# Nine instead of seven gate and up pairs by Strassen's scheme, with the affine step and the sums of x moved

## The chip, the core and the metric

The kernel runs on one core of one Trainium2 chip. TensorE (PE in the profile) multiplies matrices; VectorE (DVE), ScalarE (ACT) and GpSimd (POOL) work element by element; SyncE (SP), and also ACT and POOL, issue DMA transfers. Each engine works through its own instructions strictly in the order in which the program gives them, and waits for the others by semaphores. The metric is device time in microseconds (us) of one execution. The kernel before took 955.36, 956.61 and 959.73 us in three runs, median 956.61.

## The reference

Two decoder layers work on 512 tokens of width 1024 in float32. Layer 0 mixes tokens by causal pooling, layer 1 by differential attention; each mixer is followed by a gated feed-forward block (FFN) with an inner width of 2816:

```python
for i in range(DEPTH):                                   # DEPTH = 2, ALPHA = sqrt(2)
    h = pooling(x) if i % 2 == 0 else diff_attention(x)
    x = layernorm(ALPHA * x + h, ln_mix_g[i], ln_mix_b[i])
    y = (silu(x @ w_gate[i]) * (x @ w_up[i])) @ w_down[i]
    x = layernorm(ALPHA * x + y, ln_ffn_g[i], ln_ffn_b[i])
```

`layernorm` subtracts the mean, divides by the spread, multiplies by a factor per column and adds a shift per column. The last two are the affine step.

## The kernel before, in words

**Products.** Each float32 operand is split into a high part, rounded to the reduced format fp32r, and a low part, the remainder. A product is then three matmuls: high by high, high by low and low by high. The high part is a cast on ACT, the low part a subtraction on DVE, so each block of weights costs one operation on each of the two engines before PE can use it.

**Stages.** Pooling mixer, gate and up stage of FFN 0, its down stage, attention, then gate and up and the down stage of FFN 1. Below, "FFN 0" and "FFN 1" are the two blocks.

**Gate and up stage.** The inner width of 2816 is 22 blocks of 128 columns, and these form 11 pairs k = 0 to 10: blocks k and k + 11. A *plain* pair takes four products of 24 matmuls with 512 columns each (function `plain`, one call for each half of the pair). A pair by Strassen's scheme in Winograd's form (function `strassen`) cuts the pair in quarters and takes seven products P1, Q5, P6, Q3, P7, P2, Q4 of 24 matmuls with 256 columns each. They accumulate in three PSUM banks A, C and B; since later products are added into the same bank, ACT copies the bank out in between (bank A after P1 and after P6, bank C after Q5), and the copy must be done before PE writes that bank again: C for Q3, A for P6 and P7. Strassen's scheme needs sums of weight blocks (DVE, line 569) and of four quarters of x (`sums_of_x`: sums on DVE at 614, 629, 631, 634 and 638, casts on ACT at 617, low parts on DVE at 620, in the tile `xs`). `SPLIT` lists the pairs done in this way: 4 to 10, seven of eleven.

**Start of the stage.** The first 3 blocks (FFN 0) or 2 blocks (FFN 1), called `early`, are computed in two halves of 256 tokens, since the second half of x is still being transposed and split when PE starts (`late`). `advance` prepares weights ahead of PE; there are six buffers for split weights and five for raw ones.

**What else DVE and ACT do in this stage.** `gated` multiplies silu(gate) by up (600, 601); `affine` (200, 201) applies factor and shift of the previous layer norm to the residual rows `res`, as two operations on 128x1024 for each of the four token blocks; `sum_hidden` forms sums of the activations for the down stage (700 to 709); `weight_sums` forms sums of down weights. For the last: for each row of terms k, `load_terms` loads two transfers and one that adds on landing, all on POOL's queue (668, 669), DVE adds twice (674, 675) and ACT's queue writes the result back to memory (679); `load_terms(k + 2)` may start only after that write, since it uses the same tile. The tile of rows 3, 5, 7, 9 and 10 has the tag `gb`, which it shares with the factors and shifts of the layer norm; row 1 uses free rows of the tile `hid`.

**Down stage.** It also runs by Strassen's scheme: seven products P1, Q5, P6, Q3, P7, P2, Q4 of six items each. `prepare` keeps the splitting of weights (d_j for item j, 0 to 41) five items ahead of PE and that of the left operands (into `xs`, a subtraction at line 737 first in product P6) four ahead; then `multiply` issues the item's matmuls, and `add_to` adds each finished product to `res`.

## Time and profile before

| | |
|---|---|
| three timed runs | 955.36, 956.61, 959.73 us |
| the profiled execution: its span, first to last instruction | 952.5 us |
| median of the runs above that span | 4.1 us |
| PE, DVE, ACT, POOL busy in the span | 935.5, 780.4, 490.3, 118.0 us |
| FFN 0: gate and up, from PE's first matmul to its last | 36.4 to 269.5 us |
| FFN 0: down stage, first six products begin and end | 269.5 to 359.3 us |
| FFN 1: gate and up | 606.5 to 836.9 us |

A row of a timeline reads: start and duration in us, engine, line, operation, tiles (output<-inputs), shape, and in brackets the idle time of the engine before the instruction with what ended it. Operations are pipelined, so that the next one of the same engine can start a little before the printed duration is over; what an instruction adds to a busy engine is the distance of the starts. A table of stretches gives for each stretch its length, then for each engine the busy time and in parentheses the number of instructions. In the rows of transfers the last number is the time from issue to landing.

### The profile page before, as it was taken

The page shows a single profiled execution, that of the slowest core. Times are in us where ns is not written, and L with a number is a line of the kernel's source. Part 1 is how long each engine was busy: PE and PEld are TensorE (multiplying, and loading weights), DVE is VectorE, ACT ScalarE, POOL GpSimd, SP SyncE. Part 2 cuts the span into 40 slices and gives each one's busy share as a digit, 9 for nine tenths or more (in the row PEclk, how much of TensorE's full clock was granted, in tenths as well). Part 3 has the DMA queues.
Part 4 walks back from the last instruction along what each step waited for, and adds up shares of the span by engine and source line. Part 5 has one row for each costly group of instructions (what it writes and reads, how often), then busy time and mean ns, then how long its engine had stood idle before and what let it go on. Part 6 is the DMA issues. An engine that isn't in the chain of part 4 may idle for free.

```text
span 952.5 us, 15381 instructions
## 1 busy us (share of the span) xinstructions
PE 935.5 (98%) x5986; PEld 847.0 (89%) x5986; DVE 780.4 (82%) x1134; ACT 490.3 (51%) x788; POOL 118.0 (12%) x148
## 2 busy tenths in 40 slices
PE   8899999999999999999999999999999999999995
PEld 8898899999988888988888888998899999988884
DVE  7859979999988677688777677789779999987777
ACT  6743335555554467665556553833345554654460
POOL 4311211110001201000000000311211110001102
PEclk9999999999999999999999999999999999999998
DMA  9387988875877964333232222396888785868942
GB/s 249 131 275 236 329 254 277 257 238 212 269 244 267 368 223 134 107 89 100 74 126 79 65 89 89 121 321 214 272 240 264 240 281 200 260 242 288 357 136 89
DMA packets 82776, 197.90 MB, mean 208 GB/s; under 512 B 14820, under 2 KB 26724, under 8 KB 82702
## 3 DMA queue, kind: packets, MB, share of 16 engines
q1 hardware_dynamic: 42908, 115.09, 36.5%
q0 software_dynamic: 16192, 47.19, 17.9%
q10 hardware_dynamic: 23602, 34.63, 9.9%
q8 instruction: 47, 0.77, 0.3%
q14 instruction: 27, 0.22, 0.1%
HBM read 159.64 MB, written 36.72 MB: 206 GB/s over the span
## 4 chain that ended last, share of the span: by engine, by line
PE 92%; DVE 3%; ACT 2%; POOL 1%; issue 1%; DMA 1%; POOLq 0%; DVEq 0%
PE A L823 17%; PE P L889 13%; PE C L823 8%; PE Q L889 6%; PE B L823 4%; PE u L127 3%; PE u L125 3%; PE u L126 3%; PE g L126 3%; PE g L127 3%; PE g L125 3%; PE s L1079 2%; PE v L125 2%; PE v L127 2%; PE v L126 2%; PE q L126 2%
## 5 line engine op out<-in xcount | busy, mean ns | idle before, releaser
L569 DVE TENSOR_TENSOR raw<-raw,raw 128x1024 f32<-128x1024 f32 x56 | 68.3, 1219 | 0.5
L107 ACT CAST xs<-hid 128x512 fp32r<-128x512 f32 (+1 forms) x60 | 34.7, 581 | 24.4 <-DVE hid L737 24.4
L219 ACT ACTIVATE y<-pt,bT,gT 128x128 f32<-128x128 f32 x96 | 36.1, 456 | 21.0 <-PE pt L208 19.9
L108 DVE TENSOR_TENSOR xs<-hid,xs 128x512 fp32r<-128x512 f32 (+1 forms) x60 | 38.4, 642 | 7.8 <-ACT xs L107 7.8
L1089 ACT ACTIVATE p<-p,mn 128x128 f32<-128x128 f32 (+3 forms) x64 | 35.3, 553 | 14.9 <-DVE mn L1084 14.9
L601 DVE TENSOR_TENSOR hid<-sg,u 128x512 f32<-128x512 f32 x16 | 11.0, 686 | 29.5 <-PE u L127 18.8
L668 POOL DMA_DIRECT2D b<-in_wall x20 | 14.0, 705 | 170.6 <-DMA tsum<-b 111.0
L729 POOL DMA_DIRECT2D xs<-ssum x24 | 17.4, 726 | 142.7 <-PE Q L889 69.0
L108 DVE TENSOR_TENSOR xt<-y,xt 128x512 fp32r<-128x512 f32 x24 | 16.2, 687 | 16.9 <-ACT xt L107 16.7
L108 POOL TENSOR_TENSOR sql<-sq,sqh 128x512 fp32r<-128x512 f32 x7 | 9.0, 1290 | 165.3 <-ACT sqh L107 165.3
L668 POOL DMA_DIRECT2D hid<-in_wall x24 | 18.8, 827 | 77.5 <-DVE g_36l L575 23.6
L1084 DVE CUSTOM_DVE_ANT_0 p<-s,bias 128x128 f32<-128x128 f32 (+3 forms) x64 | 28.1, 486 | 0.0
L171 POOL TENSOR_SCALAR rs<-mv 128x1 f32<-128x1 f32 x16 | 7.8, 488 | 162.0 <-DVE mv L169 162.0
L705 ACT CAST v<-u 128x512 fp32r<-128x512 f32 x22 | 13.6, 620 | 26.9 <-DVE u L703 26.8
L163 DVE BATCH_NORM_STATS2 st<-res 128x6 f32<-128x512 f32 x32 | 22.2, 694 | 1.1
L849 ACT ACTIVATE sg<-sg 128x512 f32<-128x512 f32 x14 | 8.9, 633 | 26.0 <-DVE sg L842 26.0
L108 DVE TENSOR_TENSOR heads<-k,heads 128x512 fp32r<-128x512 f32 x8 | 5.5, 692 | 20.2 <-ACT heads L107 20.2
L669 POOL DMA_DIRECT2D hid<-in_wall x12 | 14.8, 1235 | 58.5 <-DMA hid<-in_wall 52.3
L617 ACT CAST xs<-hid 128x1024 fp32r<-128x1024 f32 x8 | 8.4, 1050 | 23.9 <-DVE hid L634 11.6
L1103 DVE SCALAR_TENSOR_TENSOR p<-p,sm,p 128x128 f32<-128x128 f32 (+3 forms) x32 | 17.7, 552 | 1.1
L838 DVE TENSOR_TENSOR hid<-C,hid 128x512 f32<-128x512 f32 x14 | 9.7, 691 | 10.8 <-PE C L823 9.6
L107 ACT CAST heads<-k 128x512 fp32r<-128x512 f32 x8 | 4.7, 588 | 26.3 <-PE k L127 26.3
(1118 smaller groups left out, 3742.4 us busy)
## 6 DMA issues: line engine op xcount, KB each, us to landing
raw<-in_wall SPq DMA_DIRECT2D x122, 512.0 KB, 4.5
r<-tsum SPq DMA_DIRECT2D x40, 512.0 KB, 4.4
hid<-in_wall POOLq DMA_DIRECT2D x36, 512.0 KB, 7.2
b<-in_wall POOLq DMA_DIRECT2D x30, 512.0 KB, 5.8
r<-in_wall SPq DMA_DIRECT2D x30, 512.0 KB, 4.9
tsum<-hid ACTq DMA_DIRECT2D x24, 512.0 KB, 5.6
ssum<-v ACTq DMA_DIRECT2D x22, 512.0 KB, 4.0
tsum<-b ACTq DMA_DIRECT2D x20, 512.0 KB, 4.9
```

Of the source, the lines that this page charges most:

```text
L107: nc.scalar.copy(dst_h, src)
L108: (low or nc.vector).tensor_tensor(dst_l, src, dst_h.bitcast(F32), op=ALU.subtract)
L125: nc.tensor.matmul(acc, ah, bh, start=start, stop=False)
L126: nc.tensor.matmul(acc, ah, bl, start=False, stop=False)
L127: nc.tensor.matmul(acc, al, bh, start=False, stop=stop)
L219: nc.scalar.activation(y[:, k, :], pt[:, k * P : (k + 1) * P], AF.Identity, bias=bT[:, n, kk : kk + 1], scale=gT[:, n, kk : kk + 1],)
L569: tt(t, raws[pair[0]], raws[pair[1]], op=ALU.add)
L668: nc.gpsimd.dma_start(out=t[:, j], in_=src[:, j])
L823: nc.tensor.matmul(o, w[:, c], x[:, kk, :], start=p in ("P1", "Q5", "P2") and f + kk + e == 0, stop=p in ("Q4", "Q3", "P2") and (f, kk, e) ...
L889: nc.tensor.matmul(accs[s], x[:, k, r], y[:, c], start=first and k == 0 and e == 0, stop=last and k == m - 1 and e == 2, skip_group_check= ...
L1084: nc.vector.tensor_tensor_reduce(out=p, in0=accs[c][:, :w], in1=biases[h][:, w - 1 :: -1] if w < S else biases[h][:, ::-1], op0=ALU.add, o ...
L1089: nc.scalar.activation(p, p, AF.Exp, bias=mn[:, q, c : c + 1], scale=-1.0, accum_out=sm[:, q, c : c + 1],)
```

## The change

Three things change, in both FFN blocks.

1. `SPLIT` becomes 2 to 10: pairs 2 and 3 are now done by Strassen's scheme too, nine of eleven.
2. `sums_of_x` is now stepped from the start of the stage, beside the first products, and ahead of the last splits of x. Row 1 of the terms moves from `hid` to the tile with the tag `gb`. At the start, the weights are now prepared to block 6 in both FFN blocks (before: 6 in FFN 0, 4 in FFN 1).
3. The affine step leaves the gate and up stage. In the down stage each half block of `res` (128x512) is multiplied by the factor (`gained`) before the first product is added to it, and gets the shift, with the factor ALPHA where that is still to come, at a later place (`shifted`): eight operations of each kind for each FFN block. The factors and shifts of the layer norm before the FFN are loaded at the end of the gate and up stage; those that attention uses are loaded at its start, and for the last layer norm a second time, on POOL's queue, after the last shift.

```diff
-SPLIT = (4, 5, 6, 7, 8, 9, 10)
+SPLIT = tuple(range(2, HALF))
...
                 whole(r2, 0, 0)
-                yield
                 whole(r3, 0, 1)
                 yield
                 whole(r0, 1, 0)
...
-                if k == 1:
-                    t = rows_of[:, :, 4:6, :]
-                elif k % 2 == 0 and k < HALF - 1:
+                if k % 2 == 0 and k < HALF - 1:
                     t = rows_of[:, :, 9:11, :]
...
                         if not lo:
-                            advance(2 * early, True)
+                            advance(6, True)
+                            if (f, i) != (0, 0 if final else 1):
+                                next(sums, None)
                     if lo:
                         advance(2 * f + 6)
                         gated(order[f], *accs[f])
-                        affine(n - 1, f)
                         catch_up()
+                        next(sums, None)
                         if f < 2:
                             weight_sums()
-                            next(sums)
...
                 gated(order[f], *a)
-                if f < SB:
-                    affine(n - 1, f)
                 if f in (3, 5, 7):
                     weight_sums()
-                if f == 3:
-                    load_terms(3)
...
-            load_gb(n)
+            load_gb(n - 1)
...
+            def gained(s, d):
+                c = slice(d * 512, (d + 1) * 512)
+                tt(res[:, s, c], res[:, s, c], gbs[n - 1][:, 0, c], op=ALU.mult)
+
+            def shifted(s, d):
+                c = slice(d * 512, (d + 1) * 512)
+                added = s < 2 or d == 1
+                nc.vector.scalar_tensor_tensor(
+                    res[:, s, c], gbs[n - 1][:, 1, c], ALPHA if added else 1.0, res[:, s, c],
+                    op0=ALU.mult, op1=ALU.add,
+                )
+
+            gains = {
+                ("P1", 1): [(0, 0)], ("P1", 3): [(1, 0)],
+                ("Q5", 0): [(2, 1)], ("Q5", 1): [(3, 1)], ("P6", 3): [(0, 1)], ("P6", 4): [(1, 1)],
+                ("P7", 3): [(2, 0)], ("P7", 4): [(3, 0)],
+            }
+            shifts = {
+                ("Q3", 0): [(0, 1)], ("Q3", 1): [(1, 1)], ("Q3", 2): [(2, 1)], ("P7", 0): [(3, 1)],
+                ("P7", 1): [(0, 0)], ("P7", 2): [(1, 0)], ("P7", 3): [(2, 0)], ("P7", 4): [(3, 0)],
+            }
...
                     multiply(j, accs, range(2))
+                    for s, d in gains.get((p, i), ()):
+                        gained(s, d)
+                    for s, d in shifts.get((p, i), ()):
+                        shifted(s, d)
+                if final and p == "P7":
+                    load_gb(n, nc.gpsimd)
...
+            load_gb(n - 1)
             load_bias(0)
...
-                if h == SB + 1:
-                    load_gb(n)
```

How the instructions now stand, at the three places of which the prediction speaks. In the changed file the same operations have other line numbers: sums of x 613, 627, 629, 632, 636 with low parts at 619 (before 614, 629, 631, 634, 638 and 620), the gated product 600 (601), additions of terms 670 and 671 (674, 675), and the two new operations 890 and 895.

DVE in FFN 0, beside the first products. Before, from the low parts of the weights of blocks 4 and 5 (g_4l, g_5l) over the last four splits of x (xt<-y) to the first gated product:

```order
L575 TENSOR_TENSOR g_4l<-raw_334,g_4h 128x1024
L575 TENSOR_TENSOR g_5l<-raw_378,g_5h 128x1024
L108 TENSOR_TENSOR xt<-y_2_0_621,xt 128x4x128
L108 TENSOR_TENSOR xt<-y_2_1_628,xt 128x4x128
L108 TENSOR_TENSOR xt<-y_3_0_669,xt 128x4x128
L108 TENSOR_TENSOR xt<-y_3_1_676,xt 128x4x128
L601 TENSOR_TENSOR hid_535<-sg_0_803,u_0_540 128x512
L200 TENSOR_TENSOR res<-res,gb_528 128x1024
L201 TENSOR_TENSOR res<-res,gb_528 128x1024
```

And now, from the same place behind g_5l:

```order
L613 TENSOR_TENSOR hid_532<-xt 128x1024 x2
L108 TENSOR_TENSOR xt<-y_2_0_621,xt 128x4x128
L108 TENSOR_TENSOR xt<-y_2_1_628,xt 128x4x128
L108 TENSOR_TENSOR xt<-y_3_0_669,xt 128x4x128
L108 TENSOR_TENSOR xt<-y_3_1_676,xt 128x4x128
L613 TENSOR_TENSOR hid_532<-xt 128x1024 x2
L627 TENSOR_TENSOR hid_532<-hid_532 128x1024
L629 TENSOR_TENSOR hid_532<-hid_532 128x1024
L632 TENSOR_TENSOR hid_532<-hid_532 128x1024
L619 TENSOR_TENSOR xs_533<-hid_532,xs_533 128x1024
L636 TENSOR_TENSOR hid_532<-hid_532 128x1024
L619 TENSOR_TENSOR xs_533<-hid_532,xs_533 128x1024
```

Two sums of x now stand ahead of the last splits of x; six sums and two of the four low parts stand between those splits and the first gated product (line 600), which is the next row.

ACT at the first pair by Strassen's scheme, pair 4 before. From the copy of bank A after P1 to its copy after P6; g_nh are casts of weights, v a cast of `sum_hidden`:

```order
L832 COPY sg_4_0_1369<-A_4_1342 128x512
L572 CAST g_21h<-raw_1183 128x1024
L572 CAST g_22h<-raw_1067 128x1024
L679 DMA tsum_537<-hid_535 128x2x512 x2
L834 COPY hid_535<-C_4_1343 128x2x256
L572 CAST g_23h<-raw_1222 128x1024
L705 CAST v_3_1388<-u_3_1387 128x2x256
L836 COPY hid_535<-A_4_1342 128x2x256
```

And now, pair 2:

```order
L824 COPY sg_2_0_1065<-A_2_1038 128x512
L571 CAST g_13h<-raw_878 128x1024
L571 CAST g_14h<-raw_573 128x1024
L705 DMA ssum_535<-v_0_968 512x1x256
L675 DMA tsum_534<-hid_532 128x2x512 x2
L826 COPY hid_532<-C_2_1039 128x2x256
L571 CAST g_15h<-raw_943 128x1024
L701 CAST v_1_1085<-u_1_1084 128x2x256
L828 COPY hid_532<-A_2_1038 128x2x256
```

The same operations stand ahead of the copy of bank C, and one more transfer issue (ssum<-v).

DVE in the down stage of FFN 0, from item 5: d_jl is the low part of the weights of item j, xs that of a left operand. Before:

```order
L108 TENSOR_TENSOR d_5l<-r_5_2912,d_5h 128x512
L108 TENSOR_TENSOR d_6l<-r_6_2946,d_6h 128x1024
L108 TENSOR_TENSOR xs_536<-hid_535,xs_536 128x256
L108 TENSOR_TENSOR d_7l<-r_7_2979,d_7h 128x1024
L108 TENSOR_TENSOR xs_536<-hid_535,xs_536 128x512
```

And now:

```order
L108 TENSOR_TENSOR d_5l<-r_5_3088,d_5h 128x512
L890 TENSOR_TENSOR res<-res,gb_3200 128x512
L108 TENSOR_TENSOR d_6l<-r_6_3122,d_6h 128x1024
L108 TENSOR_TENSOR xs_533<-hid_532,xs_533 128x256
L108 TENSOR_TENSOR d_7l<-r_7_3155,d_7h 128x1024
L108 TENSOR_TENSOR xs_533<-hid_532,xs_533 128x512
L890 TENSOR_TENSOR res<-res,gb_3200 128x512
```

Two factors (890) are new here; two more stand ahead of d_11l and d_12l, still before the first item of product P6, and the other operations keep their order.

More of the change, by code (lines that the diff above doesn't have):

```diff
@@ L679, in sum_terms @@
                     nc.scalar.dma_start(out=dst[:, j], in_=t[:, j])
-                if k + 2 < HALF - 1 and k != 1:
+                if k + 2 < HALF - 1:
                     load_terms(k + 2)
@@ L781, in plain @@
                     ahead(j + i + 5)
-                    if f >= 3:
-                        next(sums, None)
+                    next(sums, None)
                     catch_up()
                 gated(order[f], *a)
-                if f < SB:
-                    affine(n - 1, f)
                 if f in (3, 5, 7):
                     weight_sums()
-                if f == 3:
-                    load_terms(3)
                 if f % 2:
```

7 lines of the change are left out of this document (3 added, 4 removed).

## The prediction

> **What bounds the kernel now.** I read the page's head and its chain of waits first, then the stretches, then the timelines of single engines.
>
> ```profile
> span 952.5 us, 15381 instructions
> PE 935.5 (98%) x5986; PEld 847.0 (89%) x5986; DVE 780.4 (82%) x1134; ACT 490.3 (51%) x788; POOL 118.0 (12%) x148
> ...
> PE 92%; DVE 3%; ACT 2%; POOL 1%; issue 1%; DMA 1%; POOLq 0%; DVEq 0%
> ```
>
> PE is busy for 98% of the span and makes up 92% of the chain that ends last. There is almost no idle time to win: a change is worth what it takes from PE's work, less what PE then has to wait. Three stretches of FFN 0 show PE's work, a pair by Strassen's scheme, a plain pair, and the first three products of the down stage:
>
> ```profile
> 148.55:168.71 20.16, 20.16 (x171) 20.16 (x169) 19.18 (x24) 10.33 (x13) 2.70 (x3) 1.00 0.88 264
> 84.88:106.64 21.76, 21.76 (x98) 18.02 (x97) 19.59 (x23) 9.17 (x11) 2.70 (x3) 1.00 0.66 204
> 269.51:314.42 44.91, 44.91 (x201) 37.17 (x200) 35.63 (x48) 24.93 (x35) 5.10 (x7) 1.00 0.80 268
> ```
>
> In all three PE (first pair of numbers) is busy without a gap at the full granted clock (1.00). DVE (third) has only 1.0 of 20.16 us to spare in a Strassen pair. So DVE is where a wait can arise.
>
> **The saving.** Two pairs in each of two FFN blocks change from plain, 21.76 us, to Strassen, 20.16 us: 4 x 1.60 = **6.4 us**. It is PE's own work and cannot be hidden. By single matmuls: 96 of 512 columns at 226.7 ns against 168 of 256 columns at 120.0 ns.
>
> [...]
>
> **Entry of FFN 0.** Strassen's first pair now starts at block 4 instead of block 8, and the sums of x must be ready by then. These rows carry the walk along DVE, ACT and PE:
>
> ```profile
> 53.59 0.69 DVE L108 TENSOR_TENSOR xt<-y,xt 128x512 fp32r<-128x512 f32 x1 [1.37 <-ACT xt L107]
> ...
> 65.70 0.69 DVE L674 TENSOR_TENSOR hid<-hid 128x512 f32<-128x512 f32 x1
> 66.43 0.69 DVE L675 TENSOR_TENSOR hid<-hid 128x512 f32<-128x512 f32 x1
> 67.04 1.22 DVE L614 TENSOR_TENSOR hid<-xt 128x1024 f32<-128x1024 f32 x1
> 68.17 1.22 DVE L575 TENSOR_TENSOR g_6l<-raw,g_6h 128x1024 fp32r<-128x1024 f32 x1
> ...
> 81.16 0.42 DVE L700 TENSOR_TENSOR u<-hid 128x256 f32<-128x256 f32 x1
> ...
> 82.76 1.22 DVE L575 TENSOR_TENSOR g_10l<-raw,g_10h 128x1024 fp32r<-128x1024 f32 x1
> ...
> 87.30 1.22 DVE L629 TENSOR_TENSOR hid<-hid 128x1024 f32<-128x1024 f32 x1
> 88.55 1.23 DVE L631 TENSOR_TENSOR hid<-hid 128x1024 f32<-128x1024 f32 x1
> ```
> ```profile
> 49.34 1.51 ACT L219 ACTIVATE y<-pt,bT,gT 128x128 f32<-128x128 f32 x4 [1.04 <-DVE xt L108]
> ...
> 53.58 1.28 ACT L600 ACT_TABLE_LOAD   x1
> 59.77 0.60 ACT L600 ACTIVATE sg<-g 128x512 f32<-128x512 f32 x1 [4.91 <-PE g L127]
> ...
> 88.55 1.05 ACT L617 CAST xs<-hid 128x1024 fp32r<-128x1024 f32 x1 [4.11 <-DVE hid L629]
> ```
> ```profile
> 58.13 0.28 PE L125 MATMUL g<-xt,w2h 128*128 128x256 f32 x1
> ```
>
> From start to start DVE needs 1.14 us for 128x1024 (1.25 where it needs the result just before), 0.61 for 128x512 (0.73 likewise), 1.6 for the four sums of `sum_hidden`. Two sums ahead of the splits of x delay these by 2.27, also through ACT, whose y waits for DVE (row 49.34): the last starts at 53.59 + 2.27 = 55.86 and ends at 56.55. PE reads it from 58.13; no wait.
>
> Then come the other sums: from 56.47 to the end of the last sum 1.13 + 3 x 1.25 + 2 x 1.14 + 1.22 = 8.4, so 64.85; ACT casts it (1.05), loads its table, hidden before (1.28), and does the first silu (0.60). The first gated product starts at 67.85. Up to the addition of terms of row 2, DVE has 11 operations of 128x1024, nine of 128x512 and the four of `sum_hidden`, 11 x 1.14 + 9 x 0.61 + 2 x 0.12 + 1.6 = 19.9 us, and waits some 1.3 for the third silu, which stands behind three casts on ACT: it gets there at 67.85 + 21.2 = **89.0**. The affine steps that stood here (2.4 us each, three up to this place) are no longer in the count; without that the sums of x would come later still.
>
> Row 2 must have landed by then:
>
> ```profile
> 65.61 0.40 ACTq L679 DMA_DIRECT2D tsum<-hid  x1
> 71.09 0.74 POOL L668 DMA_DIRECT2D hid<-in_wall  x1 [6.79 <-DVE g_7l L575]
> hid<-in_wall POOLq DMA_DIRECT2D x2, 512.0 KB, 8.3
> hid<-in_wall POOLq DMA_DIRECT2D x1, 512.0 KB, 7.6
> ```
>
> These are the write of row 0, the loads of row 2 that follow it, 5.5 us later, with their landing (8.3 us) and that of the transfer that adds (7.6). ACT now issues the write behind two casts after the first silu, at 69.8, so the loads go at 75.3, land at 83.6, and the adding one lands at **91.2**. DVE waits 2.2. What stands behind it on ACT:
>
> ```profile
> 98.11 0.60 ACTq L709 DMA_DIRECT2D ssum<-v  x1
> 99.42 1.41 ACTq L679 DMA_DIRECT2D tsum<-hid  x1
> 131.86 0.37 ACTq L679 DMA_DIRECT2D tsum<-hid  x1
> 132.32 0.46 ACTq L679 DMA_DIRECT2D tsum<-hid  x1
> 134.35 0.59 ACT L834 COPY hid<-C 128x512 f32<-128x512 f32 x1 [0.35 <-PE C L823]
> ```
> ```profile
> 84.88 0.39 PE L125 MATMUL g<-xt,g_8h 128*128 128x512 f32 x1
> 131.43 2.88 PE C L823 x24
> ```
>
> Two additions and one sum of weights end at 91.2 + 0.73 + 0.61 + 1.22 = 93.8; the cast g_14h waits for it, and behind it stand three issues (0.60 + 0.37 + 0.46) and the copy of bank C (0.59): 95.8. PE wants bank C for Q3 three products after 84.88, at 93.5: it waits 2.3. The copy of A for P7, behind four operations on DVE and a cast, then comes 0.1 late. From there on the pairs repeat what pairs 4 to 10 did without a wait: a wait of PE gives DVE and ACT the same time back, so it is paid once. Row 3, written after the third silu (82.2), loads at 87.7 and lands at 87.7 + 8.3 + 7.6 = 103.6; DVE adds it after pair 2's last product, past 107. Its cover is 3 us. **Entry of FFN 0: 2.4 us.** Bounds: 0.2 if row 2 is in time, 4.4 if both issues take 1.41.
>
> [...]
>
> **Entry of FFN 1.**
>
> ```profile
> 617.19 0.69 DVE L108 TENSOR_TENSOR xt<-y,xt 128x512 fp32r<-128x512 f32 x1 [1.37 <-ACT xt L107]
> ```
> ```profile
> 620.36 0.28 PE L125 MATMUL g<-xt,w100h 128*128 128x256 f32 x1
> ...
> 652.23 0.39 PE L125 MATMUL g<-xt,g_8h 128*128 128x512 f32 x1
> ```
>
> Here the sums of x stand behind the splits, but the casts of blocks 4 and 5 now stand ahead of the last one; at 1.05 each they delay it from 617.19 to 619.3 at most. It is over at 620.0, and PE reads it from 620.36. From 619.3 to the first Strassen pair are 32.9 us; in FFN 0 from 55.86 to 84.88 only 29.0. These 3.9 us more exceed the 2.4 lacking there: **0**, at most 2.4 if the same transfers are later here.
>
> **The affine step in the down stage.** Sixteen operations of 0.61 for each block. The shifts stand in Q3 and P7, where DVE is ahead. Four factors stand before P6, where it is not:
>
> ```profile
> 279.62 1.23 DVE L108 TENSOR_TENSOR d_6l<-r,d_6h 128x1024 fp32r<-128x1024 f32 x1 [0.26 <-ACT d_6h L107]
> ...
> 305.67 0.69 DVE L108 TENSOR_TENSOR xs<-hid,xs 128x512 fp32r<-128x512 f32 x1 [0.69 <-ACT xs L107]
> ```
> ```profile
> 307.62 0.39 PE L889 MATMUL P<-d_15h,xs 128*128 128x512 f32 x1
> ```
> ```profile
> 269.30 0.33 SPq L150 DMA_DIRECT2D gb<-in_lng  x1
> DMA to landing us min/median/max: 4.4/4.9/6.8
> ```
>
> The left operand of item 15 is ready at 306.36 and used at 307.62, 1.26 of slack. Four factors delay it by 2.44, of which d_6l's wait takes 0.26: PE waits **0.9 us in each block, 1.8** in all. Bounds: 0, if other waits of DVE on ACT take the delay, and 2.4 each. The factors are issued at 269.30 and landed by 276.1; the first is used where d_6l's wait began, at 279.3, so there are 3.2 us of cover, DVE with everything that PE needs next would stand behind it, and what exceeds it would cost one for one. The second load for the last layer norm is issued after P7; P2 lies between, 66 x 226.7 ns = 15.0 us, against 8.3. Attention's load now stands on SP ahead of the position bias instead of behind it; both are small beside the time until DVE uses them, and I count 0.
>
> **Sum.** -6.4 + 2.4 + 0 + 1.8 = -2.2, so the span of 952.5 becomes 950.3. The 4.1 us by which the median of the runs, 956.6, exceeds that span stay: **954.4 us**.
>
> **Rivals.**
> 1. *Row 2 lands in time.* The entry costs 0.2: 952.2. For it: DVE's arrival and the landing are only 2.2 apart. Against: both landings are this kernel's own.
> 2. *Nothing waits.* 956.6 - 6.4 = 950.2. It also needs the slack of item 15 to hold; DVE waits 0.69 on ACT there at every item.
> 3. *Every cover is short by its upper bound*: -6.4 + 4.4 + 2.4 + 4.9 = +5.3, 961.9; partial forms lie between 955 and that.
> 4. *Slower: five raw buffers pace Strassen's new pairs.* Three raw blocks must be there at once, the third being fetched only when g_6l frees a buffer.
>
> ```profile
> raw<-in_wall SPq DMA_DIRECT2D x122, 512.0 KB, 4.5
> ```
>
> g_6l ends near 72.1, so this block lands at 76.6 and is summed at 78.6: 2.0 of cover. It decides from 6.5 us of landing on; at the 8.3 of POOL's loads it costs 1.8 here and as much in the next pair, in both blocks: 954.4 + 7.2 = 961.6. Against: 4.5 is the median of 122.
>
> **Chances.** Forecast 0.45, rivals 0.18, 0.20, 0.10, 0.07. A measurement of this kernel can tell about 0.5%, 4.8 us: faster means under 951.8, slower over 961.4. Rival 2 and a part of rival 1 are faster, 0.28; rival 4 and the end of rival 3 slower, 0.09; the rest, 0.63, the same. The range 949.8 to 958.6 leaves out the upper part of rivals 3 and 4 and the lowest tail.
>
> **What would show it.** Pairs 2 and 3 take 20.16 us of PE's work each. PE waits for ACT's copy of bank C (or A) in pair 2 of FFN 0, about 2.4, and for DVE's xs at item 15 of each down stage, about 0.9; nothing at FFN 1's entry. DVE's addition for row 2 waits about 2 for POOL's transfer. The forecast is wrong if waits appear in later Strassen pairs, if a factor waits for its load, or if pairs 2 and 3 cost other than 20.16.

## The result, and the profile after

| | kernel before | changed kernel |
|---|---|---|
| median of the runs | 956.57 us (9 runs, 954.55 to 960.30) | 951.95 us (9 runs, 951.00 to 954.14) |
| ratio, 95% interval | | 0.995 (0.9935 to 0.9965) |
| profiled execution: span | 952.5 us | 950.5 us, its own time 952.29 |
| PE, DVE busy in the span | 935.5, 780.4 us | 933.1, 818.6 us |

The changed kernel is 4.6 us faster, at the edge of what was called measurable beforehand (4.8): by the prediction's bounds 951.95 is still "the same", 0.15 above "faster", though the interval excludes no change. The forecast was 954.4 (949.8 to 958.6): the sign and the range held, the middle was 2.4 us too high. The page of the changed kernel, its head and its chain of waits:

```profile
span 950.5 us, 16048 instructions
PE 933.1 (98%) x6274; PEld 857.9 (90%) x6274; DVE 818.6 (86%) x1190; ACT 507.5 (53%) x812; POOL 119.0 (13%) x150
...
PE 84%; DVE 9%; ACT 3%; issue 2%; POOL 1%; DMA 1%; ACTq 0%; POOLq 0%; DVEq 0%
```

PE is still busy for 98% of the span, but DVE's share of the chain has gone from 3 to 9%: there are places now where DVE sets the pace.

**Two executions that start alike.** The two profiled spans differ by 2.0 us, the medians by 4.6. Part of this lies ahead of everything that the change touches. These rows of the stretches (granted clock: third number from the end) are of the kernel before, of the changed kernel, and of the changed kernel in a second trace (the run after_2 below):

```profile
10.00:15.00 5.00, 5.00 (x41) 4.65 (x40) 3.67 (x7) 3.52 (x6) 2.55 (x2) 1.00 1.08 356
40.00:42.00 2.00, 2.00 (x19) 2.00 (x18) 1.97 (x4) 1.60 (x5) 0.00 (x0) 1.00 0.00 0
```
```profile
10.00:15.00 5.00, 5.00 (x27) 4.60 (x26) 2.73 (x5) 2.24 (x4) 2.51 (x2) 0.66 1.07 379
40.00:42.00 2.00, 2.00 (x12) 2.00 (x11) 1.97 (x4) 1.97 (x4) 0.00 (x0) 0.50 0.00 0
```
```profile
10.00:15.00 5.00, 5.00 (x40) 4.63 (x39) 3.65 (x7) 3.50 (x6) 2.55 (x2) 1.00 1.07 362
40.00:42.00 2.00, 2.00 (x19) 2.00 (x18) 1.97 (x4) 1.60 (x5) 0.00 (x0) 1.00 0.00 0
```

In the first trace of the changed kernel PE had the full clock neither at 10 to 15 us nor at 40 to 42. Compared by the start of one and the same product, it stood 1.6 us behind the kernel before at 36 us and 2.48 behind at 45. In the second trace it stood 0.01 behind at 55. So the second trace is the one to hold against the kernel before, from there on product by product:

| place (start of the same product) | before | after_2 | what the stretch up to here cost |
|---|---|---|---|
| first half products, 55 us | 55.01 | 55.02 | 0.0 |
| first product of down stage 0 | 269.51 | 267.69 | -3.20 for two pairs, +1.37 |
| down stage 0, behind item 15 | | 1.31 ahead | +0.51 |
| entry of FFN 1 | | 1.16 ahead | +0.15 |
| first product of down stage 1 | | 3.93 ahead | -3.20 for two pairs, +0.43 |
| down stage 1, behind item 15 | | 3.40 ahead | +0.53 |
| end of the span | 952.5 | 949.5 | +0.4 |

The columns add up: -6.4 + 1.37 + 0.51 + 0.15 + 0.43 + 0.53 + 0.4 = -3.0. The four pairs gave what they should. New waits of PE took back 3.0 us of it, in five places, and the end of the program took 0.4. The 0.15 stands in attention; both traces of the changed kernel have it, those of seven, both and both_2 do not, and its cause is open. Pair 2 and pair 3 of FFN 0 and the first three products of the down stage in after_2, which answer to the three stretches shown of before:

```profile
84.89:103.53 18.64, 17.52 (x146) 17.32 (x144) 18.45 (x23) 10.23 (x13) 3.44 (x4) 1.00 0.92 293
103.53:123.69 20.16, 20.16 (x171) 20.16 (x169) 19.61 (x24) 10.14 (x13) 2.43 (x3) 1.00 0.92 298
267.69:313.11 45.42, 45.42 (x201) 37.02 (x199) 36.41 (x51) 23.40 (x33) 5.09 (x7) 1.00 0.78 264
```

The first row holds pair 2 up to its last product, six products of 2.88 us: 17.28 of work, 1.36 of waiting. The second is one Strassen pair from last product to last product: 20.16, as in the pairs before, with 0.55 us of DVE to spare. The third is 0.51 longer than the 44.91 of before.

**Where the waits are.** First the entry of FFN 0, in four timelines of after_2: DVE's, ACT's, POOL's and PE's.

```profile
55.87 0.69 DVE L108 TENSOR_TENSOR xt<-y,xt 128x512 fp32r<-128x512 f32 x1 [1.37 <-ACT xt L107]
...
63.66 1.22 DVE L636 TENSOR_TENSOR hid<-hid 128x1024 f32<-128x1024 f32 x1
...
67.91 0.69 DVE L600 TENSOR_TENSOR hid<-sg,u 128x512 f32<-128x512 f32 x1 [1.89 <-ACT sg L599]
...
89.30 0.69 DVE L670 TENSOR_TENSOR hid<-hid 128x512 f32<-128x512 f32 x1
```
```profile
67.37 0.40 ACTq L675 DMA_DIRECT2D tsum<-hid  x1
...
71.09 0.39 ACTq L675 DMA_DIRECT2D tsum<-hid  x1
...
91.88 0.60 ACTq L705 DMA_DIRECT2D ssum<-v  x1
92.52 1.60 ACTq L675 DMA_DIRECT2D tsum<-hid  x2
94.16 0.58 ACT L826 COPY hid<-C 128x512 f32<-128x512 f32 x1 [1.23 <-PE A L815]
```
```profile
70.74 0.74 POOL L664 DMA_DIRECT2D hid<-in_wall  x1 [9.48 <-DVE hid L670]
77.06 0.72 POOL L664 DMA_DIRECT2D hid<-in_wall  x1 [5.58 <-DMA tsum<-hid]
77.78 1.26 POOL L665 DMA_DIRECT2D hid<-in_wall  x1
```
```profile
93.40 0.28 PE L815 MATMUL A<-xs,g_10l 128*128 128x256 f32 x1
94.80 0.50 PE L815 MATMUL C<-xs,g_11h 128*128 128x256 f32 x2 [1.12 <-ACT hid L826]
```

And from the view of line 665, how long the transfer that adds took to land:

```profile
DMA to landing us min/median/max: 6.7/6.7/6.7
```

The walk along DVE came true to a few tenths: last split of x at 55.87 (forecast 55.86), last sum over at 64.88 (64.85), first gated product at 67.91 (67.85), row 2's addition at 89.30 (89.0). But DVE does not wait there: the transfer that adds was issued at 77.78 and landed 6.7 later, at 84.5, not at 91.2. PE waits for bank C nevertheless, since the three issues on ACT take 0.60 + 1.60 us instead of the 1.43 assumed. It starts at 94.80 what it could have started at 93.52.

The same place in FFN 1, DVE and then PE:

```profile
654.02 0.69 DVE L600 TENSOR_TENSOR hid<-sg,u 128x512 f32<-128x512 f32 x1 [1.28 <-ACT sg L599]
...
667.94 0.68 DVE L832 TENSOR_TENSOR hid<-hid,A 128x512 f32<-128x512 f32 x1
```
```profile
668.67 0.50 PE L815 MATMUL A<-xt,g_14h 128*128 128x256 f32 x2 [0.18 <-DVE hid L832]
```

Between these two DVE rows DVE has no pause at all. It comes 0.3 us late to the subtraction that frees bank A for pair 2's last product.

And item 15 of the down stage: the loads of PE's left operand (LDWEIGHTS in the trace, 0.19 us for one; they wait for xs), and the DVE operation they wait for:

```profile
305.90 0.19 PEld L881 LDWEIGHTS P<-d_15h,xs 128*128 128x128 f32 x1 [0.37 <-ACT xs L107]
...
306.63 0.30 PEld L881 LDWEIGHTS P<-d_15h,xs 128*128 128x128 f32 x2 [0.43 <-DVE xs L108]
```
```profile
305.88 0.69 DVE L108 TENSOR_TENSOR xs<-hid,xs 128x512 fp32r<-128x512 f32 x1 [0.69 <-ACT xs L107]
```

The high half, ACT's, is wanted by the item's first matmul, the low half, DVE's, by the third.

### The profile page after: what moved, and what is told of

It reads as the page before. It is cut to its first block, busy times and chain, and to the rows that moved or that the text cites. A ratio compares the mean times of both kernels' runs of the same rounds, so it can differ in the third digit from the quotient of the medians.

```text
span 950.5 us, 16048 instructions
## 1 busy us (share of the span) xinstructions
PE 933.1 (98%) x6274; PEld 857.9 (90%) x6274; DVE 818.6 (86%) x1190; ACT 507.5 (53%) x812; POOL 119.0 (13%) x150
## 4 chain that ended last, share of the span: by engine, by line
PE 84%; DVE 9%; ACT 3%; issue 2%; POOL 1%; DMA 1%; ACTq 0%; POOLq 0%; DVEq 0%
PE A L815 20%; PE P L881 13%; PE C L815 10%; PE Q L881 6%; PE B L815 5%; PE s L1098 2%; PE v L125 2%; PE v L126 2%; PE v L127 2%; PE q L126 2%; PE q L127 1%; PE q L125 1%; PE k L125 1%; PE k L127 1%; PE k L126 1%
## 5 line engine op out<-in xcount | busy, mean ns | idle before, releaser
L568 DVE TENSOR_TENSOR raw<-raw,raw 128x1024 f32<-128x1024 f32 x72 | 87.8, 1219 | 0.6
L664 POOL DMA_DIRECT2D b<-in_wall x24 | 18.0, 799 | 162.3 <-DMA tsum<-b 93.5
L841 ACT ACTIVATE sg<-sg 128x512 f32<-128x512 f32 x18 | 11.4, 632 | 33.5 <-DVE sg L834 33.5
L664 POOL DMA_DIRECT2D hid<-in_wall x20 | 14.8, 740 | 96.6 <-DMA tsum<-hid 31.2
L826 ACT COPY hid<-C 128x512 f32<-128x512 f32 x18 | 10.6, 586 | 26.8 <-PE C L815 22.9
L665 POOL DMA_DIRECT2D b<-in_wall x12 | 14.7, 1229 | 59.2 <-DMA b<-in_wall 52.7
L830 DVE TENSOR_TENSOR hid<-C,hid 128x512 f32<-128x512 f32 x18 | 12.4, 690 | 10.1 <-PE C L815 8.5
L1098 PE MATMUL s<-heads 64*128 64x256 f32 (+2 forms) x192 | 17.9, 330 | 0.0
```

What stands on the lines that cost most here:

```text
L568: tt(t, raws[pair[0]], raws[pair[1]], op=ALU.add)
L664: nc.gpsimd.dma_start(out=t[:, j], in_=src[:, j])
L1098: nc.tensor.matmul(accs[c][:, :wide], a[r, qs], b[r, :wide], start=i == 0, stop=i == 2)
```

## The experiments

All of them compute the whole reference. Kernels measured together shared the runs of the kernel before, whose median was 955.8 to 956.6 each time.

**Seven pairs again (seven).** What is worth how much: the pairs, or the work that was moved for them?

```diff
-SPLIT = tuple(range(2, HALF))
+SPLIT = tuple(range(4, HALF))
```

> The changed kernel with Strassen's scheme for pairs 4 to 10 only, as before; the moved affine steps, the moved sums of x and the moved loads stay. Theory A (the whole gain is PE's own work in the four pairs, less 0.5 and 0.4 of new waits in pair 2 of the two FFN blocks; the moved steps gain nothing by themselves): it loses 6.4 and wins back 0.9, 5.5 above the changed kernel, 957.4 us, and about 1.0 slower than the kernel before by the waits at item 15. Rival B (a good part of the gain comes from the moved work, the pairs only make use of the room): about 953 to 955, faster than before.

956.87 us, 1.001 of before (0.9998 to 1.0022). Against the changed kernel PE lost 2.66 us in FFN 0 and 2.77 in FFN 1, 5.43 together, which is 6.4 less the waits of 0.5 and 0.4 in pair 2 that went too. In the trace that is theory A to a tenth: the moves gain nothing by themselves. The stretch of plain pair 2 in FFN 0 shows that they leave DVE (third pair of numbers) half idle there, 10.61 of 21.76 us where the kernel before had 19.59; this room is what Strassen's pairs then use:

```profile
83.22:104.98 21.76, 21.76 (x98) 18.02 (x97) 10.61 (x15) 6.22 (x8) 3.74 (x5) 1.00 1.05 346
```

**The entry's DVE work put back (work_back).** Are the moves needed at all?

```diff
                         gated(order[f], *accs[f])
+                        again(f)        # twice: res[:, f] = max(res[:, f], res[:, f])
                         catch_up()
...
                 gated(order[f], *a)
+                if f < SB:
+                    again(f)
```

> The changed kernel with as much DVE work back at the entry as the affine steps were there: after each of the first four gated products of an FFN block two operations of 128x1024 on the residual (the maximum of a value with itself, which changes nothing). The affine steps in the down stage stay. Theory A (DVE is the engine that sets pair 2, so work there is paid one for one once its idle time is used up): DVE has 4 x 2.45 = 9.8 us more ahead of row 2's addition, 1.2 of idle time to give in FFN 0 and 1.8 in FFN 1, so PE waits about 8.6 more in FFN 0 and 8 in FFN 1: 968.5 us. Rival B (the weights' casts run ahead far enough, the affine steps need not have moved): 952 to 954.

974.41 us, 1.019 (1.0176 to 1.0212). PE waited twice in pair 2 of FFN 0, and what it did between the two waits ran at half the clock (the row of the stretches behind the two of PE):

```profile
96.89 0.52 PE L823 MATMUL A<-xs,g_10h 128*128 128x256 f32 x2 [3.87 <-ACT sg L832]
...
105.70 0.80 PE L823 MATMUL C<-xs,g_11h 128*128 128x256 f32 x2 [4.18 <-ACT hid L834]
```
```profile
98.00:100.00 2.00, 2.00 (x12) 2.00 (x11) 1.97 (x2) 0.00 (x0) 0.00 (x0) 0.50 0.81 135
```

Against the first trace of the changed kernel FFN 0 lost 11.8 us and FFN 1 9.6, where 8.6 and 8 were expected. The waits themselves, 8.1 in FFN 0 and 6.6 in FFN 1, are near what theory A says; the clock behind them was in neither theory. With that much DVE work at the entry the nine pairs are 18 us slower than the kernel before: moving the affine steps is what makes them pay. (About 1 of the 18 us is item 15's, since the affine steps stay in the down stage too.)

**The sums of x put back (sums_back).** The same question for the other move, in FFN 0 alone.

```diff
                         if not lo:
                             advance(6, True)
-                            if (f, i) != (0, 0 if final else 1):
+                            if final and (f, i) != (0, 0):
                                 next(sums, None)
...
                         catch_up()
                         next(sums, None)
+                        if not final:
+                            next(sums, None)
```

> The changed kernel with all sums of x of FFN 0 behind its gated products again, two portions after each of the first three and the last one in block 3; FFN 1 stays. Theory A (DVE's queue sets pair 2): 11.9 us of DVE work move from ahead of the first gated product to behind it, the first gated product itself comes some 6.5 us earlier since no cast stands ahead of its silu, 1.2 of idle time are used up, so PE waits about 4 us more in pair 2 of FFN 0, and the clock that is granted after such a wait costs another 1 to 2: 956 to 958. Rival B (the place of the sums is indifferent, only their end counts): 952 to 952.5.

960.03 us, 1.005 (1.0033 to 1.0068). DVE came to row 2's addition at 96.23 (89.30 in after_2, where PE stands within half a us of this run). PE waited 2.94 and 2.90 us in pair 2 and ran at half the clock behind each wait (0.50 from 96 to 98 and from 102 to 104 us). Against after_2, which starts alike, FFN 0 lost 7.9 us. Theory A in kind; both its terms, 4 and 1 to 2, were too small (4.5 more waiting and some 3.3 of clock), the clock's above all, since it was paid twice.

**Row 2's terms made late (row2_late).** Does the chain of the prediction hold, from the landing over DVE and ACT to PE?

```diff
-                for j in range(2):
+                for j in (0, 1, 0, 1) if k == 2 else (0, 1):
                     nc.gpsimd.dma_start(out=t[:, j], in_=src[:, j])
```

> The changed kernel with the two loads of row 2's terms issued twice, one after the other, in both FFN blocks, so that the transfer that adds comes later; the result is the same. In the changed kernel that transfer landed at 85.7 and DVE came to the addition at 90.9, 5.2 later. Theory A (the prediction's chain holds, only the landing was misjudged): two more loads of 4 to 6 us each put the landing at 94 to 97, DVE waits 3 to 6 us there, and PE waits the same for bank C: 3 to 6 us more in FFN 0, 955 to 958 with a like wait in FFN 1 up to 961. Rival B (DVE makes up the wait before PE needs bank C): 952 to 953 with DVE waiting but no longer gap of PE.

956.65 us (951.68 to 960.49). In the profiled execution the last transfer landed at 92.0, and these rows of DVE, PE and the stretches follow:

```profile
92.00 0.69 DVE L670 TENSOR_TENSOR hid<-hid 128x512 f32<-128x512 f32 x1 [2.18 <-DMA hid<-in_wall]
```
```profile
97.61 0.57 PE L815 MATMUL C<-xs,g_11h 128*128 128x256 f32 x2 [3.50 <-ACT hid L826]
```
```profile
98.00:100.00 2.00, 2.00 (x11) 2.00 (x11) 2.00 (x3) 1.55 (x3) 0.00 (x0) 0.50 1.00 202
```

DVE waits 2.18, as long as was forecast for the changed kernel itself, and PE 3.50 where after_2 had 1.12, 2.4 more: the chain holds link by link. What follows costs 1.6 us on top: the product behind the wait takes from 97.61 to 102.08, 4.47 us instead of 2.88. In FFN 1 the doubled loads still landed in time, and PE waits as little as in the changed kernel. The shortest run, 951.68, is as short as the changed kernel's own. So the forecast's entry of 2.4 was the price of a lateness that the changed kernel does not have in its two traces.

**Four raw buffers (raws4).** The prediction's fourth rival.

```diff
-RAWS = 5
+RAWS = 4
```

> The changed kernel with four raw buffers instead of five, which fetches each raw block later. It tests the prediction's fourth rival, that the buffers pace Strassen's new pairs. Theory A (the buffers have room to give: nothing in the trace of the changed kernel waits for a raw block in pairs 2 and 3): less than 2 us more, 952 to 954. Rival B (the fetch of the third block of a pair decides, 2.0 us of cover by the prediction): every Strassen pair waits, 18 pairs with 1 us or more, 970 or more.

957.78 us, 1.0025 (1.0009 to 1.0041): neither theory's number. One DVE sum in pair 2 of FFN 0 waits for a raw block, and PE behind it; the other Strassen pairs show no gap that the changed kernel does not have. A second wait stands in the last down stage. DVE and PE in pair 2:

```profile
102.64 1.23 DVE L568 TENSOR_TENSOR raw<-raw,raw 128x1024 f32<-128x1024 f32 x1 [2.54 <-DMA raw<-in_wall]
```
```profile
105.65 0.51 PE L815 MATMUL A<-xt,g_14h 128*128 128x256 f32 x2 [2.02 <-DVE hid L832]
```

Against the first trace of the changed kernel PE lost 2.4 us in pair 2 (1.6 against after_2, whose start is the nearer one), 1.9 late in the last down stage, and some 1.0 in smaller waits of the two down stages. Five buffers cover the new pairs, and in pair 2 of FFN 0 one less is too few: the rival's mechanism exists, at one place, and at five buffers it does not decide.

**The factors twice (factors_twice).** Is item 15's wait DVE's queue, one for one?

```diff
                     for s, d in gains.get((p, i), ()):
                         gained(s, d)
+                        if p in ("P1", "Q5"):
+                            z = res[:, s, d * 512 : (d + 1) * 512]
+                            tt(z, z, z, op=ALU.max)
```

> The changed kernel with each of the four factors ahead of P6 followed by one more operation of 128x512 on the same half row (the maximum of a value with itself, which changes nothing): 4 x 0.61 = 2.44 us more DVE work ahead of item 15's left operand in each down stage. Theory A (DVE runs there without a pause, so PE waits one for one): the wait of 0.52 grows to 2.96 in each stage, 4.9 us in all, 956.8. Rival B (the 0.52 is the handover from ACT, not DVE's queue): within 1 us of the changed kernel.

958.87 us (957.41 to 962.38). PE lost 2.90 and 2.92 us more in the two down stages, where 2.44 each were put in. The delay shows at item 12 already and grows to item 15, whose row has

```profile
313.12 0.50 PE L881 MATMUL P<-d_15h,xs 128*128 128x512 f32 x1 [1.02 <-ACT xs L107]
```

One for one, and some 0.1 us for each left operand that PE waits for: the matmul at 313.12 is followed by the next 0.34 us later, the same one in both, which waits for nothing, 0.23 later (306.75 to 306.98). Theory A. The median is 2.1 us above its 956.8; 0.9 of that lies in these stages, the rest is not explained by the trace, whose own execution (961.73) came to 45 us later than any other.

**Three edits of order (both), the same and one more (held).** Can the new waits be had back by order alone?

```diff
-                ("Q5", 0): [(2, 1)], ("Q5", 1): [(3, 1)], ("P6", 3): ...
+                ("P6", 2): [(2, 1), (3, 1)], ("P6", 3): ...     # Q5's additions right behind these
...
-                yield                      # sum_terms, ahead of the writes
+                for _ in range(1 + later): yield                # later = 1 for row 2
...
-                    catch_up()             # plain(f), second half
-                gated(order[f], *a)
+                gated(order[f], *a)
+                catch_up()
```

> The changed kernel with three edits of order: Q5's additions to the residual and their two factors stand behind the left operand of item 17 instead of ahead of that of item 15; the write of row 2's sums is issued one product later on ACT; the gated product of block 3 stands ahead of the steps that catch up instead of behind them. Theory A (the new waits are DVE's and ACT's order at three places, 0.5 us at item 15 in each down stage, 0.5 in pair 2 of FFN 0, 0.4 in that of FFN 1): all of them go, 1.9 us less than the changed kernel, 950.1. Rival B (PE waits for the same thing a product later, since DVE is busy throughout there): within 0.5 of the changed kernel, with new waits at Q3's first items or in pair 3.

949.98 us, 0.994 (0.9929 to 0.9952). Against the first trace of the changed kernel PE gained 0.51 at item 15 in each down stage, 0.43 in FFN 1's pair 2, all of both, but only 0.13 in FFN 0's, where 0.40 were left, 0.31 of it now in front of the last product. The edit in held, on top of these, starts the sums of block 1's hidden rows behind the subtraction that frees bank A instead of ahead of it:

```diff
-                if f % 2:
+                if f % 2 and k != 1:
                     behind.append(sum_hidden(k))
...
+                    if k == 2 and p == "P7":
+                        behind.append(sum_hidden(1))
```

> The kernel with the three edits of order (both) and one more: the sums of block 1's hidden rows, five DVE operations of 2.2 us together with their wait, start in pair 2 behind the subtraction that frees bank A instead of ahead of it. Theory A (the 0.3 us that PE still waited in pair 2 of FFN 0 are DVE's queue alone): this wait goes too, 949.7 us, no gap of PE over 0.35 us in pair 2 of either block. Rival B (DVE only pays later): a gap of the same size in pair 3.

952.20 us, 0.9966 (0.9953 to 0.9978). The wait in pair 2 is gone in both blocks, and the same wait stands in pair 3, larger, in both:

```profile
125.10 0.50 PE L818 MATMUL A<-xt,g_21h 128*128 128x256 f32 x2 [0.45 <-DVE hid L835]
```

Rival B. DVE has 0.55 us to spare in such a pair; 2.2 us that are put off from one pair come due in the next.

**Side by side (after_2, both_2), and with matmuls in PE's early waits (hot).**

```diff
-        for i in range(11):
+        for i in range(15):                      # the first warming matmuls
...
+            if layer == 0:
+                for _ in range(5):
+                    nc.tensor.matmul(accs[0][0][:, 0:P], ident, ident, start=True, stop=True)
```

> The changed kernel once more, beside the two below on the same chip. Two things are read from it: its time beside theirs, 951 to 953 us, and a second trace of the same program. Theory A (the first 45 us differ from execution to execution by the clock that PE is granted there, and this is why the profiled span of the changed kernel was only 2.0 us shorter than that of the kernel before and not 4.5): PE comes to the same product at 45 us up to 2.5 us earlier or later than in the first trace, with the granted clock below 1.00 in the stretches 10 to 15 us or 36 to 44 us where it comes late, and from there to the end the distances repeat to 0.3 us. Rival B (the 2.5 us belong to the change): the same delay again.

> The kernel with the three edits of order, once more, beside the changed kernel. Theory A: its trace showed 1.8 us less waiting behind the first 45 us, so its time is 1.8 below that of the changed kernel in the same call, 950 us. Rival B (the 2.0 us between the two medians were another day's chip): within 0.5 us of it.

> The same three edits, and matmuls whose results nobody reads in two of PE's early waits: four more of the first warming ones at the start, and five ahead of FFN 0's first product, into a bank that this product starts anew. Theory A (the clock falls to half where PE has waited, and the early waits do this in most executions): the granted clock stays at 1.00 in the stretches 10 to 15 and 36 to 44 us, 1 to 2 us less than without, 948 to 949, and less spread. Rival B (what counts there is the data that come late, or the matmuls added stand in the way): no less than without, or up to 1 us more.

Changed kernel 951.75 (950.17 to 954.69), three edits 949.45 (948.45 to 950.90), with the matmuls besides 950.68 (949.39 to 952.32). after_2 bears out theory A in its first half: the first 45 us are no part of the change. It is wrong in that the rest repeats to 0.3 us: pair 2 of FFN 0 waited 1.36 here and 0.53 in the first trace, where PE came 2.5 us later and DVE, at row 2's addition, only 1.6. The three edits are 2.3 below the changed kernel, measured side by side. The matmuls added gained nothing that can be seen. Their clock stayed at 1.00 in both stretches, but so it did in after_2 and both_2, so this execution does not say whether they hold it. In both_2, which starts as early as after_2, PE waits in pair 2 of FFN 0 again, in two places:

```profile
96.64 0.50 PE L818 MATMUL A<-xs,g_12h 128*128 128x256 f32 x2 [0.30 <-ACT hid L831]
...
103.10 0.51 PE L818 MATMUL A<-xt,g_14h 128*128 128x256 f32 x2 [0.44 <-DVE hid L835]
```

1.16 us in all, hardly less than after_2's 1.36, and hot, which starts as early, waits 1.17: with an early start DVE's queue decides there, and these edits of its order do not help. A third wait of both_2 stands at item 33 of the last down stage, 0.8 us in all, for a left operand's low half, made by DVE:

```profile
915.61 0.73 PE L884 MATMUL P<-d_33h,xs 128*128 128x512 f32 x2 [0.52 <-DVE xs L108]
```

So these two traces end only 0.4 us apart (949.5 and 949.1). hot, with the same three edits and without that wait, ends at 947.6, which is nearer to what the medians say.

**The affine steps of P7 moved into Q3 (tail).** In both_2 the span ends 12.2 us behind the start of PE's last matmul (936.86 of 949.1; before: 941.38 of 952.5, 11.1). From d_27 in the last down stage DVE had no pause to the end of the program, apart from the layer norms' own waits for POOL; ahead of it it had waited for casts of late loads, in after_2 and then both_2:

```profile
889.77 1.23 DVE L108 TENSOR_TENSOR d_25l<-r,d_25h 128x1024 fp32r<-128x1024 f32 x1 [1.28 <-ACT d_25h L107]
892.42 1.23 DVE L108 TENSOR_TENSOR d_26l<-r,d_26h 128x1024 fp32r<-128x1024 f32 x1 [1.43 <-ACT d_26h L107]
894.88 1.23 DVE L108 TENSOR_TENSOR d_27l<-r,d_27h 128x1024 fp32r<-128x1024 f32 x1 [1.23 <-ACT d_27h L107]
```
```profile
894.78 1.23 DVE L108 TENSOR_TENSOR d_27l<-r,d_27h 128x1024 fp32r<-128x1024 f32 x1 [2.93 <-ACT d_27h L107]
```

That DVE's queue sets the end shows in a constant distance: in both, both_2, held and hot the span ends 54.3 us behind the start of d_27l on DVE (894.05, 894.78, 895.85, 893.32), though PE's last matmul stands 11.1 to 12.2 us ahead of the end. How far PE is ahead does not depend on its early start alone: in hot PE's last matmul comes earliest of all, at 936.53, and the end is 11.1 behind it; d_27l waited 1.45 us for its cast there and 2.93 in both_2.

The edit fills these waits, on top of the three edits of order:

```diff
-                ("P7", 3): [(2, 0)], ("P7", 4): [(3, 0)],                    # factors
+                ("Q3", 3): [(2, 0)], ("Q3", 4): [(3, 0)],
...
-                ("Q3", 0): [(0, 1)], ("Q3", 1): [(1, 1)], ("Q3", 2): [(2, 1)], ("P7", 0): ...  # shifts
+                ("Q3", 0): [(0, 1)], ("Q3", 1): [(1, 1), (2, 1)], ("Q3", 2): [(3, 1), (0, 0)],
+                ("Q3", 3): [(1, 0), (2, 0)], ("Q3", 4): [(3, 0)],
```

> The three edits of order (as in both) and, in both down stages, the five shifts and the two factors of product P7 moved into Q3's items, where DVE waited 1.2 to 2.9 us for each of the casts of d_25 to d_27. In the traces of the changed kernel DVE has no pause from d_27 in the last down stage to the end of the program, and where PE comes early the span ends up to 1.1 us later behind PE's last product (12.2 against 11.1 us). Theory A (DVE's queue, filled by the moved affine steps, sets the end of the program in the fast executions): 4.6 us less on it there, PE's last product and the end of the span are 10.9 to 11.1 apart again, and the time is 0.5 to 1.5 below that of the three edits, 948 to 949. Rival B (the casts' weights come late from memory and PE waits for them with or without the shifts): within 0.5 us of 949.5 to 950, with the gap of PE at d_33 still there in some executions.

948.59 us (948.32 to 950.27), 0.9925 of before (0.991 to 0.994): the lowest median, but against the kernel before, measured together, no better than both_2 (0.9923). PE's last matmul starts at 937.79 of 948.3, 10.5 ahead of the end, and DVE has pauses again, waiting for ACT or PE:

```profile
904.78 1.23 DVE L108 TENSOR_TENSOR d_32l<-r,d_32h 128x1024 fp32r<-128x1024 f32 x1 [1.23 <-ACT d_32h L107]
...
922.58 0.69 DVE L871 SCALAR_TENSOR_TENSOR res<-res,P 128x512 f32<-128x512 f32 x1 [0.49 <-PE P L884]
```

So DVE's queue no longer sets the end alone, which is theory A's mechanism. The size of the gain is not shown. This execution starts 2.4 us late, like both's (1.9 late), where the distance was 11.1: 0.5 us are gone, not 1.1, and no trace of this edit starts early, where both_2's 12.2 stood. The times do not tell 948.6 from 949.5 either, since the runs overlap.

## Why the prediction was right, and where it was not

**The saving of 6.4: right.** A Strassen pair took 20.16 in the new places too, and seven lost 5.43 = 6.4 - 0.97.

**Entry of FFN 0, 2.4: the mechanism was right in its second half, wrong in the first; 1.4 with an early start, 0.5 with a late one.** The failing step is "ACT now issues the write behind two casts after the first silu, at 69.8, so the loads go at 75.3, land at 83.6, and the adding one lands at 91.2". The first half of row 0's write went right behind the silu, at 67.4; each half of row 2's load waits only for its own half of the write (the first was issued at 70.74, ahead of the second write at 71.09); the halves landed in 5.1 and 3.9 us, not 8.3; and the adding transfer needs the first half alone, so it was issued 0.7 behind the second load. Four small steps, each taken at its dear end, made 6.7 us. That was rival 1 (row 2 lands in time). That its 952.2 is the result within 0.3 is luck: it lacks 1.2 here, 0.55 at FFN 1's entry and in attention and 0.4 at the end, and has 0.8 too much in P6 and 1.6 outside the span. It gave 0.2 for the rest of this entry, and the rest was 1.4: here the size of the three issues on ACT was off, 2.20 for 1.43, and DVE stood 0.3 later. Why the loads were quicker was not tested. (Beside row 2's loads in before the trace shows reads of one other kind, five loads of raw blocks issued one after the other from 69 to 84 us, and two writes.) Row 3 landed in time too, at 107.7 for an addition at 110.8, the 3 us of cover that were forecast, but by other terms: its adding transfer took 14.3 us (12.7 in the first trace). The memory's traffic in after_2 was down there: 127 GB/s from 65 to 75 us, 265 and 236 in the two halves of the same stretch before.

**Entry of FFN 1, 0: 0.4.** The step "These 3.9 us more exceed the 2.4 lacking there" compared only with row 2. Row 2 was in time; what was late by 0.3 is DVE's own queue, begun 1.28 late since ACT's silu stood behind an issue. With the three edits of order it is gone; that the one that puts the gated product first did it was not tested alone.

**P6, 0.9 in each block: 0.5 in each.** DVE's delay was right, 2.03 where 2.18 were forecast (306.57 against 306.36 for the same low half, with the stage's begin 1.82 earlier). The failing step is "is ready at 306.36 and used at 307.62, 1.26 of slack". The low half, the one that DVE makes, is first read by the item's third matmul, 0.45 later: 1.71 of slack, 0.32 of wait, and 0.2 for the two operands waited for, some 0.1 each (305.90 to 306.24, 0.34 us where 0.23 stand in both).

**Shifts "in Q3 and P7, where DVE is ahead": right in down stage 0, not in the last.** There DVE goes on into the last layer norms with nothing behind it to hide, so the end waits for DVE where its casts come late: 0.4 us in after_2, 1.1 in both_2, nothing in hot. None of the steps priced this.

**The 4.1 us outside the span "stay": 2.45 with an equal start.** An execution's own time exceeded its span by 1.8 (952.29 to 950.5). The other 2.3 us of the 4.1 were most likely the early start of the profiled execution of before, 952.5 + 1.8 = 954.3 against the median of 956.6; there is no second trace of that kernel to show it. With its chain PE's, it should pay a late start in full, as seven did, which carried its 1.5 us to its last item with nothing added but item 15's waits (2.55 there). The changed one pays less: with a start 2.46 us later its span was only 1.0 longer (950.5 to 949.5), since pair 2's wait shrank from 1.36 to 0.53 and the tail's by 0.6. So the medians differ by 4.6 and two equal starts by 3.0. Of the 2.4 us by which the forecast was too high, 1.6 lie here and 0.8 in the sum: 1.0 and 0.8 too much at the entry of FFN 0 and in P6, less 0.4, 0.15 and 0.4 that it lacked at FFN 1's entry, in attention and at the end. These errors cancel in part, and that is luck.

**The rivals.** Nothing waits (950.2): no, PE waits in five places more. Every cover short (961.9): no; loads of factors, reloads and FFN 1's transfers were in time. Raw buffers (961.6): not at five.

## What to carry to other kernels

A stage's DVE queue is a budget: before work is put into it, count what is left of it until the next point at which the bounding engine waits, and count slack to the matmul that really reads the late half, not to the first of its group. Work put off inside a full stretch came due in the next one here (held: 0.31 us of wait gone from pair 2, 0.45 new in pair 3); what shows as a gain in the trace was moving it to where the engine waits for something else. When two profiles are compared, first find a product ahead of the change and see whether both stand at the same time there.

## What the runs showed of the hardware that was not expected

**A wait of PE cost more than itself.** Behind waits of 2.9 to 4.7 us (sums_back, work_back, row2_late) the granted clock was 0.50: 10 to 12 matmuls of 256 columns stand in 2 us there, against 18 to 20 at 1.00. In row2_late, where no other wait followed, the next product of 2.88 us took 4.47, 1.6 more. Behind the 1.1 us of after_2 the clock stayed at 1.00. Behind the 2.0 of raws4 no fall shows either: by the mean clock of that execution, 0.994 against 0.996 in after_2, the one near 40 us is the only one that fits (an estimate: 0.002 of 955.6 us are 3.8 us at 0.50). How long the low clock lasted is worked out here from the mean clock of stretches of 2 us, with 0.50 as the low value: 3.4 us (row2_late, 96 to 102 us: 0.97, 0.50, 0.67; sums_back, 94 to 100: 0.74, 0.50, 0.91, and 100 to 106: 0.95, 0.50, 0.70), or twice that (work_back, 674 to 682: 0.52, 0.50, 0.50, 0.77, 6.8 us). The length of the wait alone does not decide: 2.90 us were enough in sums_back, and at the start of the program two waits of 1.1 and 0.3 us stood ahead of the 0.50 at 40 us in the first trace of the changed kernel, and of 1.00 in before. What else decides was not tested.

**The first 45 us vary from execution to execution.** One and the same program came to a product at 45 us 2.47 us apart in its two traces (the changed kernel) and 2.14 apart (the three edits). Thirteen other traces, of kernels that differ little up to there, were compared with that of before by the start of one product at 45 us. Where the granted clock was 1.00 from 5 to 44 us (row2_late, sums_back, after_2, both_2, hot) PE came there between 0.2 us earlier and 0.5 later; where it fell to 0.50 near 40 us alone (raws4, seven) 0.6 and 1.5 later; where it was also 0.66 to 0.69 at 10 to 15 us (the first trace, both, work_back, held, tail) 1.9 to 2.5 later; and 5.1 later in factors_twice, with 0.50 in both places. Why the clock falls in one execution and not in the other stays open.

**An issue on ACT was not free for ACT.** Two writes issued one after the other held it for 1.60 us in after_2 and 1.67 in the first trace (0.64 and 0.93 there) where the same two lines had taken 0.83 (0.37 + 0.46) in a later pair of before; its next operation in after_2, the copy of bank C, started right behind them, at 94.16 (the issues from 92.52 to 94.12). What makes an issue longer was not looked into.
